# A hybrid decoder layer: rope in two halves, the sums of w_out moved behind the attention, casts and squares placed apart

## The chip, the cores and the metric

The kernel runs on one core of a Trainium2 chip. The metric is device time in microseconds (us), the median of three runs; lower is better. One more execution was taken by the hardware profiler, and all views quoted here are of that one. Its engines are PE (TensorE: matrix products), DVE (VectorE), ACT (ScalarE), POOL (GpSimd) and SP (SyncE, which here only issues transfers); 16 DMA engines move data.

## The reference, cut to what matters

One decoder layer on x of 512 tokens by 1024 channels, in float32. Two branches run on the same normed input and are merged by gates.

```python
h    = rms_norm(x, norm_g)
proj = h @ w_in            # q | f | i | z_a | c_q | c_kv | k_rope | z_b | gate logits (2 x 1024)
y_a  = hgrn2_branch(hq, hf, hi, hz, ...)       # 8 heads of 128, chunkwise gated recurrence
y_b  = mla_branch(cq, ckv, kr, mz, ...)        # 8 heads of 128 + 64 rope, causal attention
gates  = sigmoid(glog + b_gate)                # two gates per channel
merged = gates[0] * (y_a @ w_proj_a) + gates[1] * (y_b @ w_proj_b)
out    = rms_norm(x + merged @ w_out, final_norm_g)
```

Rope turns the 64 rope channels of each query head: `[x1*cos - x2*sin, x2*cos + x1*sin]`, so the two 32-channel halves have to be exchanged.

## The kernel before, in words

**Precision.** Every float32 operand of a product is split in two float32r parts, hi and lo, and a product is made of three matmuls, hi*hi, hi*lo and lo*hi (`mm3`, lines 88 to 93). `load_w` (lines 99 to 120) brings 0.5 MB of a weight into a buffer `w_raw` by SP (line 112), ACT casts it to `w_hi` (line 118) and DVE subtracts to get `w_lo` (line 119). There are three buffers of `w_raw` and four each of `w_hi` and `w_lo`. `split` (lines 160 and 161) does the same for an operand made on the chip.

**Stages.** (1) Norm, transposes into hT, the low-rank projections cT. (2) HGRN2 in four pairs of heads (`hg_pair`): forget, value or gate, query products, then states, scores, outputs. (3) Attention, head by head (lines 904 to 934): `mla_scores`, `mla_gate`, `mla_nope` for the next head, `mla_transpose`, `mla_out`; every second head `mla_rope` for the next two. (4) Two gate products, (5) the product with `w_proj_a`, each by Strassen's scheme with seven half-size products (`strassen`, lines 871 to 895), (6) the plain product with `w_proj_b`, (7) the Strassen-like product with `w_out`, the residual and the final norm.

**Sums of weight blocks.** Strassen needs four sums of 512x512 blocks for each of the four matrices (`gate_w[0]`, `gate_w[1]`, `pa_w`, `out_w`; class `BlockSums`, lines 736 to 763). They are made in DRAM by the DMA engines alone: `start` queues eight copies of 0.5 MB from the weight to a DRAM tile (`g_t`, `pa_t`, `out_t`); `load_w` issues one of the queued copies on SP behind each weight load (lines 113 to 115, 747). `add` then issues accumulating transfers of 0.5 MB on POOL (line 754), two for each of the four sums: n = 0 and 2 add a block of the weight, n = 1 and 3 add an earlier sum. `out_t` of n = 1 therefore waits for n = 0, and n = 3 for n = 1.

**What sets the order.** Within an engine a scheduler orders the instructions by its own model of time, unless a stretch is in `manual_schedule`, which keeps the order of the code for the engines named. The list `adds` (lines 796 and 797) is popped by `step()`, 11 times in HGRN2 and once for each of heads 1 to 6 of the attention; all four matrices are started before HGRN2 (line 805). In `strassen` the work on the coming operands (`between`: `a_parts` and others) is put in with `issue_after(last_lo)` (line 877), so on DVE it stands behind the last `w_lo` of the weight just loaded.

**Rope.** `mla_rope(pair)` (lines 622 to 642) makes the product for two heads, copies it to `qr` (ACT, line 626), sends four transfers of 64 KB from ACT's queue to exchange the quarters (`qs`, line 628), multiplies and adds on POOL (lines 629 to 631), sends two transfers of 128 KB (line 635) and casts into `qp` and `qh` (lines 637 to 641). For pair 0 it is called in `first_scores` (line 815), behind the states of the last pair of HGRN2, and for pairs 1 to 3 behind the scores of heads 1, 3 and 5 (lines 908 to 910).

**End.** `squares_of` (line 1069) takes its scratch `sq` from the three `w_raw` buffers.

Of the kernel before, what the change touches and what calls it, by code (L numbers as in the profile page):

```python
# [9 lines left out]
F32 = mybir.dt.float32  # L10
# [8 lines left out]
P = 128  # L19
# [4 lines left out]
H = 8  # L24
# [10 lines left out]
WCH = 1024  # L35
# [3 lines left out]
def hybrid_layer(ctx: ExitStack, tc: tile.TileContext, a):  # L39
    nc = tc.nc  # L40
# [4 lines left out]
    wraw = ctx.enter_context(tc.tile_pool(name="wraw", bufs=3))  # L45
# [14 lines left out]
    def z_tile():  # L60
        return zpool.tile([P, S], F32, tag="z", name="z")
# [31 lines left out]
        nc.tensor.matmul(ps, ll[lsl], rh[rsl], start=False, stop=stop)  # L93

    last_dma = [None]
    last_lo = [None]
    queued = []

    def load_w(*pieces, to=None):

        raw = wraw.tile([P, WCH], F32, tag="raw", name="w_raw")
        hi, lo = to or [pool.tile([P, WCH], F32R, tag=tag, name=f"w_{tag}")[:] for pool, tag in ((whi, "hi"), (wlo, "lo"))]
        views, o = [], 0
        for src in pieces:
            n = int(np.prod(src.shape[1:]))
            if len(src.shape) == 4:
                _, k, h, c = src.shape
                dst = raw[:, o : o + n].rearrange("p (k h c) -> p k h c", k=k, h=h)
                for i in range(k):
                    nc.sync.dma_start(dst[:, i], src[:, i])  # L110
            else:
                last_dma[0] = nc.sync.dma_start(raw[:, o : o + n].rearrange("p (k c) -> p k c", k=src.shape[1]), src)
                if queued:
                    with tc.issue_after(last_dma[0].ins):
                        queued.pop(0)()
            views.append([t[:, o : o + n].rearrange("p (k c) -> p k c", k=src.shape[1]) for t in (hi, lo)])
            o += n
        nc.scalar.copy(hi[:, :o], raw[:, :o])  # L118
        last_lo[0] = nc.vector.tensor_tensor(lo[:, :o], raw[:, :o], hi[:, :o].bitcast(F32), op=ALU.subtract)  # L119
        return views[0] if len(views) == 1 else views  # L120

# [159 lines left out]
    with tc.manual_schedule(engines={mybir.EngineType.PE, mybir.EngineType.Activation, mybir.EngineType.DVE}):  # L281
# [17 lines left out]
        sq, rs = st.tile([P, D], F32, "sq", bufs=2), rss[0]  # L299
# [316 lines left out]
    def low(w, k0, nk):  # L616
        ps = mm_tile()
        for k in range(nk):
            mm3(ps[:], w, cT, (slice(None), k), (slice(None), k0 + k), k == 0, k == nk - 1)
        return ps  # L620

    def mla_rope(pair):

        ps = low(load_w(w_uq[:, :, 2 * pair : 2 * pair + 2, 128:192]), 0, 3)
        qr, qs = ma_pool.tile([P, S], F32, "qr"), ma_pool.tile([P, S], F32, "qs")
        nc.scalar.copy(qr[:], ps[:])
        for b in range(4):
            nc.scalar.dma_start(qs[32 * b : 32 * b + 32, :], qr[32 * (b ^ 1) : 32 * (b ^ 1) + 32, :])
        nc.gpsimd.tensor_tensor(qr[:], qr[:], qtab[:, 0], op=ALU.mult)
        nc.gpsimd.tensor_tensor(qs[:], qs[:], qtab[:, 1], op=ALU.mult)  # L630
        nc.gpsimd.tensor_tensor(qr[:], qr[:], qs[:], op=ALU.add)

        qx = ma_pool.tile([P, S], F32, "qs")
        for i in range(2):
            nc.scalar.dma_start(qx[64 * i : 64 * i + 64, :], qr[64 - 64 * i : 128 - 64 * i, :])
        qp, qh = [ma_pool.tile([P, S], F32R, f"qp{i}") for i in range(2)], ma_pool.tile([P, S], F32R, "qh")
        nc.scalar.copy(qh[:], qx[:])
        for i in range(2):
            own, other = slice(64 * i, 64 * i + 64), slice(64 - 64 * i, 128 - 64 * i)
            nc.scalar.copy(qp[i][own], qr[own])  # L640
            nc.vector.tensor_tensor(qp[i][other], qx[other], qh[other].bitcast(F32), op=ALU.subtract)
        return qp
# [86 lines left out]
    def minus(out, x, y):  # L729
        nc.vector.tensor_tensor(out, x, y, op=ALU.subtract)  # L730
# [34 lines left out]
    gate_w = [BlockSums(f"g{b}", w_in[:, COL_G + b * D : COL_G + b * D + D]) for b in range(2)]  # L765
    pa_w = BlockSums("pa", a["w_proj_a"][0])
    out_w = BlockSums("out", a["w_out"][0])
    h_dram = [[dram.tile([P, 4, 256], F32, name=f"h{n}{i}") for i in range(2)] for n in range(1, 5)]

    def early_sums(q):  # L770
# [9 lines left out]
        def keep(n, tag, src):  # L780
# [12 lines left out]
        minus_minus(e12, e12, e22)  # L793
        keep(4, "qn", e12)

    adds = [(gate_w[0], 0), (gate_w[0], 2), (gate_w[0], 1), (gate_w[1], 0), (gate_w[0], 3), (gate_w[1], 2), (gate_w[1], 1),
            (pa_w, 0), (gate_w[1], 3), (pa_w, 2), (pa_w, 1), (out_w, 0), (pa_w, 3), (out_w, 2), (out_w, 1), None, (out_w, 3)]

    def step():
        if adds and last_pool[0]:  # L800
            x = adds.pop(0)
            if x:
                x[0].add(x[1])

    for w in (*gate_w, pa_w, out_w):
        w.start()

    for pair in range(H // 2 - 1):
# [3 lines left out]
    early = []  # L812

    def first_scores():
        early.append(mla_rope(0))
        early.append(mla_nope(0, ma_pool))

    def last_outputs(scores, outs, gated):
# [5 lines left out]
            gated(on)  # L824
        return z

    z = hg_pair(H // 2 - 1, first_scores, last_outputs)
    hw.close()

# [41 lines left out]
    def strassen(w, ops, out, pool, first=None, between={}):  # L871

        y11, y12, y22, s1, s2, s3, s4 = ops

        def run(n):
            if n in between:
                with tc.issue_after(last_lo[0].ins):
                    between[n]()

        if first is None:  # L880
            u = ch_product(w.block(0, 0), y11, copied("c11", 1.0, pool))
            run(1)
            ch_product(w.block(1, 0), y12, closed("c11", 0, 0, 1.0, out), tile=mm_tile)
            run(2)
        else:
            u = first
        r = ch_product(w.sum(1), s1, copied("c22", -1.0, pool))
        run(3)
        ch_product(w.sum(2), s2, copied("c12", -1.0, pool), u)
        run(4)  # L890
        ch_product(w.block(1, 1), s4, closed("c12", 4, 0, -1.0, out), r)
        run(5)
        ch_product(w.sum(3), s3, closed("c22", 4, 1, -1.0, out), u)
        run(6)
        ch_product(w.sum(4), y22, lambda b, ps: out(2 * b, 1, two(ps)), u)
# [6 lines left out]
    qp, nope, pn = early  # L902
    late = None
    for h in range(H):
        pools = (ma_pool, mw)
        if h:
            pn = mla_scores(h, pools[h % 2], *nope, qp, h + 1 == H)
        if h + 1 < H:
            if h % 2:
                qp = mla_rope((h + 1) // 2)  # L910
        if h:
            z = mla_gate(h)
        if h:
            if h + 1 < H:
                nope = mla_nope(h + 1, pools[(h + 1) % 2])
            mla_out(*late)
            if h % 4 == 0:
                v = mla_values(h)
        hook = lambda: mla_transpose(pn)
        if h + 1 == H:  # L920
            with tc.manual_schedule(engines={mybir.EngineType.PE}):
                pts, later = [], []
                w11, w21 = gate_w[0].block(0, 0), gate_w[0].block(1, 0)
                u = ch_product(w11, h11, copied("c11", 1.0))
                ch_product(w21, h12, lambda b, ps: later.append((b, ps)), tile=mm_tile, hook=lambda: pts.extend(hook()))
                mla_out(h, pts, v, z)
        elif h:
            late = (h, hook(), v, z)
            step()
        else:  # L930
            with tc.manual_schedule(engines={mybir.EngineType.PE}):
                nope = mla_nope(1, pools[1])
                v = mla_values(0)
                late = (0, hook(), v, z)
# [25 lines left out]
        closed("c11", 0, 0, 1.0, gate_out(0, lambda j: ma[:, j]))(b, ps)  # L960
    h_ops = (h11, h12, h22, s1, s2, s3, s4)
    y11, y12, y21, y22 = blocks(ya)
    with tc.manual_schedule(engines={mybir.EngineType.PE}):
        strassen(gate_w[0], h_ops, gate_out(0, lambda j: ma[:, j]), gp, first=u,
                 between={3: lambda: a_parts(y11, q1), 4: lambda: a_parts(y12, q2), 5: lambda: a_parts(y22, q3),
                          6: lambda: [minus(y22[:, q], y22[:, q], y21[:, q]) for q in kh]})
    g1 = {j: z_tile()[:] for j in (0, 1, 4)}
    for n, j in enumerate((2, 3, 5, 6, 7)):
        g1[j] = g_rows[:, n]
# [51 lines left out]

    sp = Pool("sums", "left")
    s1, s2 = [[sp.tile([P, 4, 256], F32R, f"s{n}{i}") for i in range(2)] for n in (1, 2)]
    fg = [z_tile() for _ in range(2)]
    with tc.issue_after(xr_in.ins):
        for n in range(2):
# [41 lines left out]

    def squares_of(t, i, o, n):

        sq = wraw.tile([P, WCH], F32, tag="raw", name="sq")
        nc.scalar.activation(sq[:, :n], xr[t][:, o : o + n], AF.Square, scale=D ** -0.5, accum_out=ssum[:, t, i : i + 1])  # L1072
        if t > 1:
            nc.vector.tensor_tensor(rgs[t - 2][:, o : o + n], xr[t][:, o : o + n], fg[o // 512][:, o % 512 : o % 512 + n],
                                    op=ALU.mult)
# [119 lines left out]
```

## Time and profile before

| | us |
|---|---|
| three runs: median (lowest to highest) | 627.75 (627.64 to 627.92) |
| the profiled execution, its own time | 626.55 |
| its span, first to last instruction | 624.8 |
| PE busy in the span | 603.7 |
| DVE / ACT / POOL busy | 431.9 / 284.6 / 147.7 |
| granted PE clock, mean | 0.996 of full speed |

The span is what the views divide up; 1.75 us of the profiled execution's time lie around it. The profile's page has the busy time of each engine, the span in 40 slices with a digit for tenths, the DMA queues (q1 is SP's, q10 ACT's, q0 POOL's), and groups of instructions. "Share of 16 engines" is the time that a queue's packets took, as a share of what 16 DMA engines have. A view of waits names who waited for whom, with total, number and longest; the view of DMA can be asked for a window. In a row of the timeline the brackets hold the idle time of the engine before the instruction and what ended it. L844 is the matmul of the Strassen products, L91 to L93 are the three of `mm3`.

### The profile page before, as it was taken

What the parts mean: (1) busy time and instruction counts of PE and PEld (TensorE: products, weight loads), DVE (VectorE), ACT (ScalarE), POOL (GpSimd) and SP (SyncE); (2) the same over time, 40 slices, a digit from 0 to 9 for tenths busy, and PEclk for the clock granted to TensorE, in tenths of its full rate; (3) what the DMA queues carried; (4) which work ended last, traced back from release to release, by engine and by line L of the source; (5) the groups of instructions that cost most, each with busy time, mean ns of one, the idle gap of its engine ahead of it and who ended that gap; (6) DMA issues with size and microseconds to landing.
All of it is one profiled execution on the core that took longest, in us unless ns stands there. A gap on an engine that the chain in (4) does not pass through costs nothing.

```text
span 624.8 us, 9801 instructions
## 1 busy us (share of the span) xinstructions
PE 603.7 (97%) x3688; PEld 526.9 (84%) x3688; DVE 431.9 (69%) x679; ACT 284.6 (46%) x531; POOL 147.7 (24%) x245
## 2 busy tenths in 40 slices
PE   8999999999999999979998999898999999999994
PEld 5998888888888888867887888798999999888883
DVE  7727989498864459838665766655766687657886
ACT  5645244323233232346555454437677844333352
POOL 3106322444341153351525213320000000000012
PEclk9999999999999999999999999999999999999998
DMA  7449479988979944937575662584656555685043
GB/s 250 166 140 335 152 244 367 277 207 183 285 128 342 220 62 116 195 98 151 96 150 121 125 161 84 135 311 162 205 170 198 194 165 183 203 302 169 1 134 135
DMA packets 74799, 114.37 MB, mean 183 GB/s; under 512 B 7512, under 2 KB 41726, under 8 KB 74752
## 3 DMA queue, kind: packets, MB, share of 16 engines
q1 hardware_dynamic: 65100, 89.69, 44.3%
q0 software_dynamic: 7952, 21.50, 19.2%
q10 hardware_dynamic: 1700, 2.56, 1.4%
q8 instruction: 29, 0.48, 0.3%
q14 instruction: 18, 0.15, 0.1%
HBM read 105.34 MB, written 39.85 MB: 232 GB/s over the span
## 4 chain that ended last, share of the span: by engine, by line
PE 78%; DVE 8%; DMA 4%; ACT 4%; issue 3%; POOL 2%; ACTq 0%; POOLq 0%; SPq 0%; DVEq 0%
PE mm_ps L91 16%; PE mm_ps L92 16%; PE mm_ps L93 16%; PE ax_ps L844 16%; PE mm_ps L844 3%; DMA qs<-qr 2%; DVE w_lo L119 2%; PE mm_ps L271 1%; PE ax_ps L687 1%; PE ax_ps L711 1%; DMA w_raw<-w_uq 1%; DVE ya L1067 1%; PE ax_ps L541 1%; PE ax_ps L91 1%; PE ax_ps L93 1%
## 5 line engine op out<-in xcount | busy, mean ns | idle before, releaser
L119 DVE TENSOR_TENSOR w_lo<-w_raw,w_hi 128x1024 fp32r<-128x1024 f32 (+3 forms) x116 | 137.1, 1194 | 91.2 <-ACT w_hi L118 85.4
L118 ACT CAST w_hi<-w_raw 128x1024 fp32r<-128x1024 f32 (+3 forms) x116 | 114.9, 1004 | 141.5 <-PE mm_ps L92 60.8
L91 PE MATMUL mm_ps<-hT,w_hi 128*128 128x512 f32 x320 | 126.0, 395 | 0.4 <-DVE qn L161 0.4
L92 PE MATMUL mm_ps<-hT,w_hi 128*128 128x512 f32 x320 | 125.1, 391 | 0.0
L93 PE MATMUL mm_ps<-hT,w_lo 128*128 128x512 f32 x320 | 124.7, 392 | 0.0
L91 PEld LDWEIGHTS mm_ps<-hT,w_hi 128*128 128x128 f32 x320 | 60.2, 188 | 12.5 <-DVE qn L161 0.6
L93 PEld LDWEIGHTS mm_ps<-hT,w_lo 128*128 128x128 f32 x320 | 60.1, 188 | 12.4
L92 PEld LDWEIGHTS mm_ps<-hT,w_hi 128*128 128x128 f32 x320 | 60.1, 188 | 11.8
L844 PE MATMUL ax_ps<-s,w_hi 128*128 128x256 f32 x384 | 54.2, 283 | 2.1 <-ACT w_hi L118 2.1
L844 PEld LDWEIGHTS ax_ps<-s,w_hi 128*128 128x128 f32 x384 | 49.6, 192 | 2.5 <-ACT w_hi L118 2.5
L1085 POOL TENSOR_SCALAR ssum<-ssum 128x1 f32<-128x1 f32 x3 | 0.9, 316 | 185.8 <-ACT sq L1072 185.8
L93 PE MATMUL mm_ps<-w_hi,hT 128*128 128x512 f32 (+1 forms) x96 | 36.6, 383 | 0.0
L92 PE MATMUL mm_ps<-w_lo,hT 128*128 128x512 f32 (+1 forms) x96 | 36.5, 382 | 0.0
L91 PE MATMUL mm_ps<-w_hi,hT 128*128 128x512 f32 (+1 forms) x96 | 36.4, 386 | 0.0
L844 PE MATMUL ax_ps<-s,w_lo 128*128 128x256 f32 x192 | 31.3, 284 | 0.2 <-DVE w_lo L119 0.2
L695 POOL TENSOR_SCALAR p<-p,sm 128x128 f32<-128x128 f32 (+3 forms) x28 | 16.8, 604 | 61.5 <-DVE sm L692 51.6
L693 ACT ACTIVATE p<-ax_ps,sm 128x128 f32<-128x128 f32 (+3 forms) x32 | 16.9, 529 | 27.7 <-DVE sm L692 26.3
L844 PEld LDWEIGHTS ax_ps<-s,w_lo 128*128 128x128 f32 x192 | 26.6, 192 | 0.4 <-DVE w_lo L119 0.4
L460 DVE RECIPROCAL tf<-pr 128x512 f32<-128x512 f32 x8 | 26.8, 3348 | 0.1
L91 PE MATMUL mm_ps<-cT,w_hi 128*128 128x512 f32 x52 | 20.7, 398 | 0.0
L93 PEld LDWEIGHTS mm_ps<-w_hi,hT 128*128 128x128 f32 x96 | 18.0, 188 | 3.0
L91 PEld LDWEIGHTS mm_ps<-w_hi,hT 128*128 128x128 f32 x96 | 18.0, 188 | 3.0
(296 smaller groups left out, 1205.5 us busy)
## 6 DMA issues: line engine op xcount, KB each, us to landing
w_raw<-w_in SPq DMA_DIRECT2D x54, 512.0 KB, 6.9
g_t<-w_in SPq DMA_DIRECT2D x16, 512.0 KB, 8.9
w_raw<-g_t SPq DMA_DIRECT2D x16, 512.0 KB, 4.2
g_t<-w_in POOLq DMA_DIRECT2D x8, 512.0 KB, 11.3
pa_t<-w_proj_a SPq DMA_DIRECT2D x8, 512.0 KB, 12.2
g_t<-g_t POOLq DMA_DIRECT2D x8, 512.0 KB, 8.3
out_t<-w_out SPq DMA_DIRECT2D x8, 512.0 KB, 8.9
s<-h POOLq DMA_DIRECT2D x8, 512.0 KB, 7.5
```

Of the source, the lines that this page charges most:

```text
L91: nc.tensor.matmul(ps, lh[lsl], rh[rsl], start=start, stop=False)
L92: nc.tensor.matmul(ps, lh[lsl], rl[rsl], start=False, stop=False)
L93: nc.tensor.matmul(ps, ll[lsl], rh[rsl], start=False, stop=stop)
L118: nc.scalar.copy(hi[:, :o], raw[:, :o])
L119: last_lo[0] = nc.vector.tensor_tensor(lo[:, :o], raw[:, :o], hi[:, :o].bitcast(F32), op=ALU.subtract)
L271: nc.tensor.matmul(ps, hT[l][:, 4 * kh + k, t * P : t * P + P], c_hl[kh][r][:, k * 256 : k * 256 + 256], start=kh == 0 and kind == 0 and k ...
L460: nc.vector.reciprocal(rp[:], pr[:])
L541: nc.tensor.matmul(ops[:, sl], asb[:, sl], v_sb[i][:, (h % 4) * P : (h % 4) * P + P], start=True, stop=i == 0)
L687: nc.tensor.matmul(sps[:, :n], qh[:, bl], kpe[x][:, :n], start=False, stop=x == 1)
L693: nc.scalar.activation(p[:, :n], sps[:, :n], AF.Exp, scale=SCALE, bias=sm[:, 1:2], accum_out=sm[:, 2:3])
L695: scaled_p = (nc.vector if final else nc.gpsimd).tensor_scalar(p[:, :n], p[:, :n], sm[:, 3:4], 0.5, op0=ALU.mult, op1=ALU.mult)
L844: nc.tensor.matmul(ps[:, o], w[k // 2][i][:, k % 2, cols], ap[j][:, k], start=not banks and c == 0 and n == 0, stop=n == 11, skip_group_ch ...
```

## The change

It has four parts.

1. `mla_rope` becomes `mla_turn(pair)` (product, copy, exchange, POOL's arithmetic, second transfers) and `mla_rope(qr, qx)` (the casts). The turn for pair 0 is issued ahead of the last pair of HGRN2; for pairs 1 to 3 ahead of the scores of heads 1, 3 and 5, and the casts behind those scores.
2. `out_w` is started only before the first gate product, so its eight copies follow the first eight weight loads of that stage, and its adds are issued behind the code of that product. `adds` is left with the eight of the gates in another order, the adds of `pa_w` are made at heads 2 (n = 0 and 2), 4 (n = 1) and 6 (n = 3).
3. The work in `between` is held behind the last cast to `w_hi` on ACT as well.
4. `sq` gets a tile of its own.

```diff
-        nc.scalar.copy(hi[:, :o], raw[:, :o])
+        last_hi[0] = nc.scalar.copy(hi[:, :o], raw[:, :o])
...
-    def mla_rope(pair):
+    def mla_turn(pair):
 
         ps = low(load_w(w_uq[:, :, 2 * pair : 2 * pair + 2, 128:192]), 0, 3)
...
         for i in range(2):
             nc.scalar.dma_start(qx[64 * i : 64 * i + 64, :], qr[64 - 64 * i : 128 - 64 * i, :])
+        return qr, qx
+
+    def mla_rope(qr, qx):
+
...
-    adds = [(gate_w[0], 0), (gate_w[0], 2), (gate_w[0], 1), (gate_w[1], 0), (gate_w[0], 3), (gate_w[1], 2), (gate_w[1], 1),
-            (pa_w, 0), (gate_w[1], 3), (pa_w, 2), (pa_w, 1), (out_w, 0), (pa_w, 3), (out_w, 2), (out_w, 1), None, (out_w, 3)]
+    adds = [(gate_w[0], 0), (gate_w[0], 2), (gate_w[1], 0), (gate_w[0], 1), (gate_w[1], 2), (gate_w[0], 3), (gate_w[1], 1),
+            None, (gate_w[1], 3)]
...
-    for w in (*gate_w, pa_w, out_w):
+    for w in (*gate_w, pa_w):
         w.start()
...
-        early.append(mla_rope(0))
+        early.append(mla_rope(*turned_q))
...
+    turned_q = mla_turn(0)
     z = hg_pair(H // 2 - 1, first_scores, last_outputs)
...
-                with tc.issue_after(last_lo[0].ins):
+                with tc.issue_after(last_lo[0].ins), tc.issue_after(last_hi[0].ins):
...
+        if h % 2 and h + 1 < H:
+            turned_q = mla_turn((h + 1) // 2)
         if h:
             pn = mla_scores(h, pools[h % 2], *nope, qp, h + 1 == H)
-        if h + 1 < H:
-            if h % 2:
-                qp = mla_rope((h + 1) // 2)
+        if h % 2 and h + 1 < H:
+            qp = mla_rope(*turned_q)
...
-            step()
+            if h % 2 == 0:
+                pa_w.add(*{2: (0, 2), 4: (1,), 6: (3,)}[h])
...
+    out_w.start()
     with tc.manual_schedule(engines={mybir.EngineType.PE}):
         strassen(gate_w[0], h_ops, gate_out(0, lambda j: ma[:, j]), gp, first=u,
...
+    out_w.add(0, 2)
+    out_w.add(1)
+    out_w.add(3)
...
+    sq = sp.tile([P, 512], F32, "sq")
...
-        sq = wraw.tile([P, WCH], F32, tag="raw", name="sq")
```

How this moves instructions, at three places. A number behind a tile's name tells buffers apart: `g_t_647` and `g_t_648` are the first and second sum of the first gate's weight, `out_t_659` to `out_t_662` the four of `w_out`, `h_663` and on the stored sums of the activations. Lines are those of each kernel's own file; L751 and L758 of the changed kernel are L747 and L754 of before, L950 is L943.

SP's queue where the first gate product begins, in the kernel before: the last load of the attention, the four loads of the two plain blocks, then the sums.

```order
L112 DMA w_raw<-w_in 128x8x128
L112 DMA w_raw<-w_in 128x2x512 x4
L112 DMA w_raw<-g_t_647 128x1024 x2
L112 DMA w_raw<-g_t_648 128x1024 x2
L112 DMA w_raw<-w_in 128x2x512 x2
L112 DMA w_raw<-g_t_649 128x1024 x2
```

The same place in the changed kernel.

```order
L112 DMA w_raw<-w_in 128x8x128
L112 DMA w_raw<-w_in 128x2x512 x4
L112 DMA w_raw<-g_t_647 128x1024
L751 DMA out_t_659<-w_out 128x2x512
L112 DMA w_raw<-g_t_647 128x1024
L751 DMA out_t_659<-w_out 128x2x512
L112 DMA w_raw<-g_t_648 128x1024
L751 DMA out_t_660<-w_out 128x2x512
L112 DMA w_raw<-g_t_648 128x1024
```

A copy of 0.5 MB now stands behind each of eight weight loads in a row; it goes on so up to the second load of `g_t_649`.

POOL's queue from the last probabilities of the attention to the end, before:

```order
L695 TENSOR_SCALAR p_3946<-p_3946,sm 128x512
L754 DMA out_t_662<-out_t_660 128x1024 x2
L943 DMA s_4339<-h_663 128x1024
L943 DMA s_4340<-h_664 128x1024
...
L943 DMA s_4344<-h_668 128x1024
L1085 TENSOR_SCALAR ssum<-ssum 128x1 x2
```

and in the changed kernel:

```order
L699 TENSOR_SCALAR p_3930<-p_3930,sm 128x512
L758 DMA pa_t_658<-pa_t_656 128x1024 x2
L950 DMA s_4323<-h_663 128x1024
...
L950 DMA s_4328<-h_668 128x1024
L758 DMA out_t_659<-w_out 128x2x512 x2
L758 DMA out_t_660<-out_t_659 128x1024 x2
L758 DMA out_t_661<-w_out 128x2x512 x2
L758 DMA out_t_662<-out_t_660 128x1024 x2
L1096 TENSOR_SCALAR ssum<-ssum 128x1 x2
```

All eight adds of `w_out` now stand behind the loads of the activations' sums, one after the other, with nothing of POOL behind them until the final norm.

ACT's queue where rope of pair 0 stands, in the last pair of HGRN2, before (`osq` are the squares of the recurrence's outputs, `kt` is of its states):

```order
L626 COPY qr<-mm_ps 128x512
L628 DMA qs<-qr 32x512 x3
L499 COPY kt<-ax_ps 128x384
L628 DMA qs<-qr 32x512
...
L635 DMA qs<-qr 64x512 x2
L640 CAST qp_2574<-qr 64x512
L640 CAST qp_2575<-qr 64x512
L118 CAST w_hi<-w_raw 128x1024
L637 CAST qh<-qs 128x512
L547 ACTIVATE osq,ss<-ax_ps 128x128 x8
```

In the changed kernel it stands ahead of the squares of the pair before, which start at 221.16 us of the profiled span, where the L626 of the rows above starts at 254.48 us (`tf` belongs to the forget gates of the last pair):

```order
L626 COPY qr<-mm_ps 128x512
L628 DMA qs<-qr 32x512 x4
L547 ACTIVATE osq,ss<-ax_ps 128x128 x8
L118 CAST w_hi<-w_raw 128x1024
L635 DMA qs<-qr 64x512 x2
L454 ACTIVATE tf<-mm_ps 128x512
L644 CAST qp_2562<-qr 64x512
L644 CAST qp_2563<-qr 64x512
L118 CAST w_hi<-w_raw 128x1024
L641 CAST qh<-qs 128x512
```

The squares of the last pair no longer stand behind the transfers and casts of rope.

More of the change, by code (lines that the diff above doesn't have):

```diff
@@ L95, in hybrid_layer @@
     last_dma = [None]
-    last_lo = [None]
+    last_hi, last_lo = [None], [None]
     queued = []
```

## The prediction

> **What bounds the kernel now.** I read the page first: busy time by engine, then the slices.
>
> ```profile
> PE 603.7 (97%) x3688; PEld 526.9 (84%) x3688; DVE 431.9 (69%) x679; ACT 284.6 (46%) x531; POOL 147.7 (24%) x245
> ...
> PE   8999999999999999979998999898999999999994
> ...
> DMA  7449479988979944937575662584656555685043
> ```
>
> PE has work in 97% of the span, and only the slices around 265, 335, 405, 425 and the end fall below 9. So whatever moves on other engines counts only where PE waits. The view of PE's waits lists them; the columns are line of PE, what released it, total us, number, longest.
>
> ```profile
> PE ax_ps L687 <- DVE qp L641: 2.5, 1, 2.5
> PE ax_ps L844 <- ACT w_hi L118: 2.1, 2, 1.6
> PE ax_ps L91 <- DVE pt L161: 1.6, 1, 1.6
> PE ax_ps L711 <- POOL p L695: 1.4, 1, 1.4
> ...
> PE mm_ps L91 <- DVE z L563: 1.1, 1, 1.1
> PE ax_ps L1033 <- DVE ya L1067: 0.8, 1, 0.8
> ...
> PE ax_ps L91 <- DVE k L549: 0.7, 1, 0.7
> ...
> PE ax_ps L844 <- DVE w_lo L119: 0.2, 1, 0.2
> ```
>
> These rows, 10.4 us together, are about all that removing waits can bring; the tail behind the last matmul is not touched. Each part of the change aims at one of them. What a part can cost is a new wait where PE has none today: the Strassen stages.
>
> **Rope of pair 0.** The chain of waits between 258 and 278 us (start, us, what):
>
> ```profile
> 258.28 8.68 DMA qs<-qr
> 267.12 1.26 POOL qr L629
> ...
> 274.43 0.61 ACT qh L637
> 275.05 0.27 ACT osq L547 x2
> ...
> 277.37 1.04 POOL ss L166
> ```
>
> The exchange of quarters takes 8.68 us, POOL's arithmetic follows, then ACT's casts, and only behind them on ACT the squares `osq`, which the last pair's outputs need. So three of PE's waits hang on this one transfer: 2.5 for `qp`, 0.7 for `k` (L549, released by the squares) and 1.1 for `z`. In the changed kernel the turn and its casts are over a whole pair earlier. All three go: 2.5 + 0.7 + 1.1 = -4.3 us. Its nine matmuls, six transfers and three POOL operations now lie in slices where PE shows 9 and the add of `pa_w` that was there is gone; ACT's second transfers wait for POOL with the tanh of the forget gates behind them, which PE's full queue hides. I take 0 for that; without the cover it would be the three operations' 3 x 1.3 = 4 us.
>
> **Rope of pair 1 and the adds at head 2.** POOL's timeline there:
>
> ```profile
> 320.16 1.68 POOL L754 DMA_DIRECT2D pa_t<-pa_t  x2
> ...
> 332.34 1.29 POOL L629 TENSOR_TENSOR qr<-qr,qtab 128x512 f32<-128x512 f32 x1 [2.70 <-DMA qs<-qr]
> ...
> 337.52 1.25 POOL L695 TENSOR_SCALAR p<-p,sm 128x384 f32<-128x384 f32 x2
> ```
>
> Two adds are issued at 320.2, rope's exchange comes behind them, POOL stands until 332.3, and probabilities queued behind rope on POOL are late: PE's 1.4 us at L711. The change puts four adds there in place of two, so the exchange has adds beside it for longer. Between -1.4 (the earlier product helps) and +4.5 (it waits about as much longer as half of another pair): I take +1.
>
> **The copies and adds of `w_out`.** Until now they ran beside HGRN2 and the attention. Taking them away there brings 0, as PE shows no wait there that they cause but those above. They come to the first gate product, whose need the view of DMA for 440 to 480 us shows (packets, MB, share of 16 engines):
>
> ```profile
> DMA packets 2803, 7.45 MB, mean 186 GB/s; under 512 B 224, under 2 KB 224, under 8 KB 2799
> ...
> q1 hardware_dynamic: 2799, 7.40, 58.7%
> ...
> w_raw<-g_t SPq DMA_DIRECT2D x8, 512.0 KB, 3.8
> ```
>
> 7.40 MB are 14.1 loads of 0.524 MB in 40 us: one in 2.83 us, with a landing time of 3.8 us, and 41% of the DMA engines left over. What an add costs stands in the same view for 145 to 169 us, where four adds (q0) met SP's queue (q1):
>
> ```profile
> q0 software_dynamic: 832, 2.10, 54.2%
> q1 hardware_dynamic: 2545, 3.79, 48.7%
> ...
> w_raw<-w_in SPq DMA_DIRECT2D x4, 512.0 KB, 13.4
> ```
>
> The engines are full (103%). Four adds took 0.542 x 24 = 13.0 us of them, 3.25 each; SP's 3.79 MB are 7.2 transfers in 11.7 us, 1.62 each; and a weight load landed after 13.4 us. In HGRN2 PE bears that: there it is four loads in 24 us, one in 6, not one in 2.83. New work in the gate stage: eight adds, 8 x 3.25 = 26.0, and six copies (the first two go out before the adds can start), 6 x 1.62 = 9.7; 35.7 us in all. In a stretch of L us the leftover 41% takes in 0.41 L. Nothing holds the adds back but their own copies and sums; at the pace of the rows above four take 24 us, so L = 48, and short are 35.7 - 0.41 x 48 = 16 us.
>
> How much of that the loads' lead covers, from ACT's and DVE's timelines and the chain:
>
> ```profile
> 453.03 2.00 ACT L118 CAST w_hi<-w_raw 128x1024 fp32r<-128x1024 f32 x2 [1.36 <-issue]
> ...
> 458.74 2.00 ACT L118 CAST w_hi<-w_raw 128x1024 fp32r<-128x1024 f32 x2 [1.50 <-PE ax_ps L844]
> ```
> ```profile
> 454.11 2.36 DVE L119 TENSOR_TENSOR w_lo<-w_raw,w_hi 128x1024 fp32r<-128x1024 f32 x2 [2.00 <-ACT w_hi L118]
> ```
> ```profile
> 459.42 5.76 PE mm_ps L844 x48
> ```
>
> The weights of the product that starts at 459.42 are ready at 456.5: 3 us of lead. The next cast is released by PE, not by its load, so the data lay ready; I allow 1.5 us more, 4.5 in all. PE then loses 16 - 4.5 = 11.5 us. The 2.3 us that PE waits here already (L844 for `w_hi` and `w_lo`) lie in the same stretch and are not paid twice: +9 us. Bounds: if the adds took only what the loads leave, -2.3; if they take as many bytes as SP's queue, an add and a transfer take 4.87 us, L is 39, short are 19.7, and it is +12.9.
>
> The Trainium skill (DMA: Bandwidth & Descriptors, "Queues, rings and completion order") says that each engine serves the queue rows in turn, one packet from each; by that rule the adds get as many turns as SP's queue, and the sum takes the upper bound, +12.9. The row has 2545 packets of SP's beside 832 of POOL's, so here the turns were not one to one over the stretch as a whole, and I keep 9.
>
> **Casts held on ACT.** ACT's timeline where PE waits for `w_hi`:
>
> ```profile
> 424.49 3.21 ACT L160 CAST q<-ya 128x512 fp32r<-128x512 f32 x6
> ...
> 428.09 1.98 ACT L118 CAST w_hi<-w_raw 128x1024 fp32r<-128x1024 f32 x2
> ```
>
> Six operand casts stand before two weight casts that PE needs. The new order would take out up to the 2.3 us; the operands themselves are wanted only in the product with `w_proj_a`, so their delay costs 0. But with loads late it is the load that PE waits for, so in my sum this brings nothing of its own.
>
> **Squares.** SP's queue waits for `sq` here:
>
> ```profile
> SPq L112 <- ACT sq L1072: 1.2, 2, 1.0
> ```
>
> The last weights come up to 1.2 us earlier, but PE's 0.8 us there is for DVE's L1067, not for a weight. Between 0 and -0.8; I take 0.
>
> **Sum.** -4.3 + 1 + 9 = +5.7 us on the profiled execution's 626.55. The median of the runs is 627.75, 1.2 above it; I add the difference to the median: 633.5 us. With the gate stage between +7 and +12 and rope of pair 1 between -1.4 and +4, this case spans 629 to 639.
>
> **Rivals.** (1) *The gate stage takes it in.* The adds yield, the copies fit between loads, and the held casts bring their 2.3: 627.75 - 4.3 - 2.3, with 1.4 more at best from pair 1 and the squares: about 620.5. For it: the 41% left over, and nobody needs the sums before the product with `w_out` 100 us later. Against it: the adds would have to stretch over (35.7 - 4.5) / 0.41 = 76 us, 19 for each pair, where the rows show 12. (2) *Half of the shortage*: adds are held up by late copies, L is about 62, short are 10, less lead and old wait +3.5; with -4.3 and +1, 628. (3) *Worse*: one turn each (+12.9), and four adds in front of pair 1's exchange (+4.5): 627.75 - 4.3 + 17.4, about 641. (4) *Rope's early half hides nothing*, because ACT or POOL makes the early place pay the same 4.3: 638.
>
> **Chances.** Likeliest case 0.40, (1) 0.30, (2) 0.12, (3) 0.13, (4) 0.05. The likeliest case alone is 629 to 639. The range reaches into (1) and (3): 620 to 641, which leaves out the better part of (1) and of (3), less than 2 in 10. A measurement of this kernel can tell about 0.2%, 1.3 us, from no change. Faster by more: (1) and a quarter of (2), 0.33; within: 0.05; slower by more: 0.62.
>
> **What would show it.** Right: no wait of PE for `qp` (L687), `k` or `z` near 275 us; in the first gate product waits of PE at L844 for `w_hi` and `w_lo` of over 8 us together, released by loads that land after 8 us or more instead of 3.8; DMA digits of 9 from about 400 to 460 us; the later stages as dense as now, only shifted. Wrong: `w_raw<-g_t` still landing near 4 us while adds run, and PE's slices at 9 there; then it is rival (1) and the time is near 620.

## The result, and the profile after

| | before | changed | 
|---|---|---|
| median of the runs, us (lowest to highest) | 627.69 (626.68 to 627.92) | 642.23 (641.72 to 647.03) |
| the profiled execution / its span, us | 626.55 / 624.8 | 642.71 / 640.8 |

The changed kernel takes 1.025 of the time of before (95% interval 1.020 to 1.030): 14.5 us slower, where 5.7 were forecast, and 1.2 us above the range. The page of the changed kernel, busy time and slices (L849 here is L844 of before, L715 is L711, L1045 is L1033):

```profile
PE 609.8 (95%) x3688; PEld 533.7 (83%) x3688; DVE 433.1 (68%) x679; ACT 285.6 (45%) x531; POOL 147.0 (23%) x245
...
PE   8999999999999999999989999947799999999994
...
PEclk9999999999999999999999999987899999999999
DMA  7549399969695523504393825999976555685123
```

The slice at 265 us is full now. The hole is at 417 to 465 us, the first gate product, where the DMA engines show four nines in a row and the granted clock falls. PE's waits say for what:

```profile
PE ax_ps L849 <- ACT w_hi L118: 16.0, 4, 7.4
PE ax_ps L715 <- POOL p L699: 2.4, 2, 1.6
...
PE ax_ps L1045 <- DVE ya L1079: 0.9, 1, 0.9
PE ax_ps L849 <- DVE part L872: 0.8, 1, 0.8
```

The waits for `qp`, `k` and `z` are gone, and 2.1 us for `w_hi` have become 16.0. The view of DMA for 415 to 460 us shows weight loads that land after 14 us, where those of the kernel before take 4.4 (408 to 449 us):

```profile
q1 hardware_dynamic: 3209, 7.66, 53.5%
q0 software_dynamic: 1604, 3.95, 50.1%
...
w_raw<-g_t SPq DMA_DIRECT2D x5, 512.0 KB, 14.2
out_t<-w_out SPq DMA_DIRECT2D x5, 512.0 KB, 18.0
```

SP's queue, which has loads and copies, and POOL's, which has the adds, each hold half of engines that are full.

**Where the time went.** PE runs the same 3688 matmuls in these kernels, near the marks used here in the same order, so their start times can be set against each other, counted from the last one. The 1380th from the end lies in the first of the seven half-size products of the first gate product, the 1080th in the last of them; worked out from the matmul starts of the two traces:

```
                       before   changed   difference so far
1380th from the end    409.77    403.99   -5.8
1080th                 449.18    465.10   +15.9
last                   616.89    632.93   +16.0
```

Up to the gates the changed kernel is 5.8 us ahead; between the two marks it loses 21.7 us (61.1 us in place of 39.4); from there to the end the gap doesn't change. The same stretch in the view by windows (its columns: window, length, busy us of PE, PEld, DVE, ACT and POOL with counts, then granted clock, DMA share, GB/s), first of the kernel before, then of the changed one:

```profile
409.77:449.18 39.41, 37.11 (x302) 36.36 (x301) 23.61 (x29) 23.68 (x38) 1.15 (x3) 1.00 0.70 236
```
```profile
403.99:465.10 61.11, 44.32 (x303) 43.01 (x301) 23.57 (x30) 22.38 (x36) 9.02 (x10) 0.83 1.03 275
```

Share times length is engine time: 0.70 x 39.41 = 27.6 us before, 1.03 x 61.11 = 62.9 us now. The new work is therefore 35.3 us; 35.7 were forecast. (Some 1.6 of the 35.3 are loads of the activations' sums, 4.19 MB behind the mark now and 3.60 before.) So the work was priced right in total, and what it costs PE was not. A share counts the time that packets took, their waiting included; whether the engines or the memory behind them are the limit, no run here separates. The clock is a second suspect: PE's busy time in the stretch is 7.2 us longer at a clock of 0.83.

### The profile page after: what moved, and what is told of

Its sections match the earlier page's. It is cut to its first block, busy times and chain, and to the rows that moved or that the text cites. A ratio compares the mean times of both kernels' runs of the same rounds, so it can differ in the third digit from the quotient of the medians.

```text
span 640.8 us, 9797 instructions
## 1 busy us (share of the span) xinstructions
PE 609.8 (95%) x3688; PEld 533.7 (83%) x3688; DVE 433.1 (68%) x679; ACT 285.6 (45%) x531; POOL 147.0 (23%) x245
## 4 chain that ended last, share of the span: by engine, by line
PE 80%; DMA 7%; DVE 5%; ACT 3%; issue 2%; POOL 2%; ACTq 1%; POOLq 0%; DVEq 0%
PE mm_ps L91 17%; PE mm_ps L92 17%; PE mm_ps L93 17%; PE ax_ps L849 14%; DMA w_raw<-w_in 3%; PE mm_ps L849 3%; DMA w_raw<-g_t 2%; DMA qs<-qr 2%; PE mm_ps L271 1%; PE ax_ps L691 1%; DVE w_lo L119 1%; PE ax_ps L541 1%; PE ax_ps L715 1%; PE ax_ps L236 1%; PE ax_ps L503 1%
## 5 line engine op out<-in xcount | busy, mean ns | idle before, releaser
L849 PE MATMUL ax_ps<-s,w_hi 128*128 128x256 f32 x384 | 59.8, 301 | 16.0 <-ACT w_hi L118 16.0
L91 PEld LDWEIGHTS mm_ps<-hT,w_hi 128*128 128x128 f32 x320 | 60.1, 188 | 12.3 <-DVE qn L161 0.6
L93 PEld LDWEIGHTS mm_ps<-hT,w_lo 128*128 128x128 f32 x320 | 60.1, 188 | 12.3
L92 PEld LDWEIGHTS mm_ps<-hT,w_hi 128*128 128x128 f32 x320 | 60.1, 188 | 11.8
L849 PEld LDWEIGHTS ax_ps<-s,w_hi 128*128 128x128 f32 x384 | 54.6, 209 | 16.8 <-ACT w_hi L118 16.8
L849 PE MATMUL ax_ps<-s,w_lo 128*128 128x256 f32 x192 | 33.2, 297 | 0.0
L699 POOL TENSOR_SCALAR p<-p,sm 128x128 f32<-128x128 f32 (+3 forms) x28 | 15.2, 545 | 65.5 <-DVE sm L696 33.2
L849 PEld LDWEIGHTS ax_ps<-s,w_lo 128*128 128x128 f32 x192 | 28.6, 206 | 0.2 <-DVE w_lo L119 0.2
L91 PE MATMUL mm_ps<-cT,w_hi 128*128 128x512 f32 x52 | 20.7, 398 | 0.0
## 6 DMA issues: line engine op xcount, KB each, us to landing
pa_t<-w_proj_a SPq DMA_DIRECT2D x8, 512.0 KB, 12.9
```

The source lines that it names most:

```text
L91: nc.tensor.matmul(ps, lh[lsl], rh[rsl], start=start, stop=False)
L92: nc.tensor.matmul(ps, lh[lsl], rl[rsl], start=False, stop=False)
L699: scaled_p = (nc.vector if final else nc.gpsimd).tensor_scalar(p[:, :n], p[:, :n], sm[:, 3:4], 0.5, op0=ALU.mult, op1=ALU.mult)
L849: nc.tensor.matmul(ps[:, o], w[k // 2][i][:, k % 2, cols], ap[j][:, k], start=not banks and c == 0 and n == 0, stop=n == 11, skip_group_ch ...
```

## The experiments

Theory at the start: the engine time in that stretch is the whole cause (A). Rivals: the order on SP's queue, each load behind a copy (Q); the clock, halved after PE's waits (C); a cost hidden in the other parts. All kernels are edits of the changed one unless another is named. For each the stretch between the same two marks is given, worked out from matmul starts as above:

```
                                      1380th   1080th   stretch
before                                409.77   449.18   39.4
changed                               403.99   465.10   61.1
part 2 undone                         408.06   445.40   37.3
no adds of w_out                      404.08   445.41   41.3
copies early, adds behind the sums    406.10   455.44   49.3
rope halves alone                     410.03   450.49   40.5
part 2 undone, casts not held         407.98   447.39   39.4
adds of the attention regrouped       409.56   446.89   37.3
```

**Part 2 undone.**

```diff
-    for w in (*gate_w, pa_w):
+    for w in (*gate_w, pa_w, out_w):
...
-            if h % 2 == 0:
-                pa_w.add(*{2: (0, 2), 4: (1,), 6: (3,)}[h])
+            step()
...
-    out_w.start()
...
-    out_w.add(0, 2)
-    out_w.add(1)
-    out_w.add(3)
```

with the list `adds` of before.

> The changed kernel with part 2 undone (w_out started before HGRN2, and the list of adds as before); the rope halves, the held casts and the tile of sq stay. Theory (the loss lies in the gate stage alone, and comes from the transfers of w_out): the gate stage's idle time (16.75 us) and PE's slower matmuls there (6.1 us more busy time) go, and 627.7 - 4.3 (rope) - 2.3 (old waits of the gate stage) give about 621, 619.5 to 623. Rival (the other parts have a cost of their own that the trace puts down to the gate stage, the held casts above all): 627 or more, with waits for w_hi at the gate stage still there.

Measured 623.48 us (622.73 to 626.83), 0.994 of before (0.992 to 0.997), half a us above the theory's range: the loss is part 2's, and this kernel beats both. It takes 37.3 us for the stretch, 2.1 less than before. But it is only 1.7 us ahead at the 1380th matmul, not 5.8; its waits have a new row:

```profile
PE mm_ps L91 <- DVE z L563: 1.8, 1, 1.8
PE ax_ps L91 <- DVE pt L161: 1.6, 1, 1.6
```

The first lies at 242 us, at the place that rope of pair 0 has moved to; the second was in the kernel before at 401.8 us. Neither is in the changed kernel. So ahead of the gates part 2 is worth 408.06 - 403.99 = 4.1 us. That is not the transfers of `w_out` alone, none of whose adds runs in HGRN2: part 2 also moves the adds of `w_proj_a` out of HGRN2, two of which are issued at 231.2 and 232.0 us here and land by 243.5, just where `z` is late. The two runs with early copies (below) have the copies of `w_out` in HGRN2 but not these adds, and no wait for `z`. The wait for `pt` goes with the order of PE's matmuls in the last head: the kernel before, this one and the others with that wait have one order there, the changed kernel and all runs without the wait another.

**No adds.** The three lines `out_w.add(...)` removed; the sums of `w_out` are left as plain blocks.

> The changed kernel without the eight adds of w_out (its sums are left as plain blocks; the eight copies between the weight loads stay). Theory A (the time of the DMA engines decides: eight adds at 3.25 us are some 26 of about 30 us that the stretch has too much): what is left, six to eight copies of 1.6 us, fits into what the loads leave, loads land after 4 to 7 us, and the time is 621 to 626. Rival Q (the order on SP's queue decides: each of eight weight loads stands behind a copy of 0.5 MB): more than half of the loss stays, 632 or more, with loads landing after 8 us or more.

Measured 622.59 us (622.19 to 623.65). The stretch, beside PE's waits in it:

```profile
404.08:445.41 41.33, 38.96 (x302) 37.91 (x301) 24.08 (x31) 22.91 (x37) 1.03 (x2) 0.96 0.91 311
```
```profile
PE ax_ps L849 <- ACT w_hi L118: 2.3, 3, 1.6
```

Eight copies stand between the loads as they did, and cost 41.3 - 37.3 = 4 us of the 61.1 - 37.3 = 23.8 that copies and adds cost together. Q falls. The copies are 0.91 x 41.33 - 0.76 x 37.34 = 9.2 us of engine time (0.76 is the share in the stretch of the kernel without part 2). The forecast has 9.7 for six of them; that its total came out is luck in this part:

```profile
408.06:445.40 37.34, 36.86 (x303) 36.31 (x301) 23.87 (x31) 23.56 (x38) 1.20 (x3) 1.00 0.76 249
```

**Filled waits.** Extra matmuls where PE waits for the second half of a weight:

```diff
+                    if n_fill and (b, c, n) == (0, 0, 2):
+                        for _ in range(n_fill):
+                            nc.tensor.matmul(idle_ps[:, o], hT[0][:, 0, 0:128], hT[0][:, 0, 0:256], start=True, stop=True)
...
+    FILL = (56, 48, 36)
```

> The changed kernel with 56, 48 and 36 extra matmuls of 128x256 (about 0.116 us each, on data that lie ready, into a bank that nobody reads) on PE in the second, third and fourth half-size product of the first gate product, where PE waits for the second half of the weight: 6.5, 5.6 and 4.2 us of work in place of idle time, so that PE is never idle for long and the granted clock should stay at 1.0. Theory A (loads set the pace there): the time stays at 641 to 644; the waits that are left and the fillers together grow as the matmuls get faster. Rival C (the halved clock costs its 6.1 us of slower matmuls on its own): 635 to 638.

Measured 645.19 us (642.16 to 648.25), far from C's 635 to 638 and 1.2 us above A's range. The changed kernel by windows of 5 us, then this one:

```profile
425.00:430.00 5.00, 0.00 (x0) 0.00 (x0) 0.00 (x0) 0.00 (x0) 0.86 (x1) 0.64 1.02 263
430.00:435.00 5.00, 3.68 (x17) 3.69 (x18) 2.43 (x3) 2.09 (x3) 0.81 (x1) 0.50 1.05 295
...
445.00:450.00 5.00, 5.00 (x25) 5.00 (x25) 2.31 (x5) 1.70 (x4) 1.13 (x1) 0.50 1.06 265
```
```profile
425.00:430.00 5.00, 5.00 (x44) 5.00 (x43) 0.49 (x1) 1.57 (x3) 0.86 (x1) 1.00 1.05 333
430.00:435.00 5.00, 5.00 (x44) 5.00 (x43) 1.94 (x3) 0.52 (x1) 0.81 (x1) 1.00 1.06 307
...
460.00:465.00 5.00, 0.72 (x3) 0.75 (x4) 3.65 (x4) 3.10 (x7) 0.00 (x0) 0.76 0.82 192
```
```profile
PE ax_ps L856 <- DVE part L880: 4.9, 1, 4.9
```

At the halved clock 25 matmuls take the 5 us that 44 take at full clock. With the fillers the clock holds at 1.00 to 460 us, and PE is done earlier only to wait longer, 4.9 us on one wait at the end of the stretch. No time is won, so C falls: while loads are late here, slow matmuls fill time that PE would stand. The 642.2 of the changed kernel lie at the lower end of this run's spread, so the fillers themselves may have cost up to 3 us.

**One product later.** `out_w.start()` and the three adds moved to the second gate product, where the loads leave more of the engines free.

> The changed kernel with the start of w_out and its adds one product later: the eight copies follow the first eight loads of the second gate product, the adds stand behind that product's code. There the kernel before keeps the DMA engines busy for 0.58 of the time (446 to 486 us), beside the first gate product for 0.71 (408 to 446 us). Theory A (what counts is the engine time that is left over, with some 30 us of new work over 55 us): PE gets (55 - 30) / 0.58 = 43 us of work done in those 55, loses about 12, less 4.5 of lead, so about 7.5 to 12 above the kernel without part 2 (about 621): 628 to 633. Rival (the adds slow a weight load by the same factor wherever they meet one): 640 or more, as now.

Measured 641.57 us (639.4 to 643.49), the rival's number: theory A in this form falls. The stretch between the marks and the next 420 matmuls (the second gate product and the first part of the product with `w_proj_a`) of this kernel, and below them the latter of the kernel without part 2:

```profile
403.98:441.39 37.41, 36.94 (x303) 36.40 (x302) 23.96 (x31) 22.81 (x37) 2.34 (x4) 1.00 0.81 270
441.39:515.19 73.80, 59.49 (x422) 58.43 (x421) 34.63 (x40) 35.80 (x57) 6.76 (x7) 0.86 0.89 233
```
```profile
445.40:495.80 50.40, 50.40 (x423) 50.40 (x421) 33.99 (x40) 34.77 (x57) 0.00 (x0) 1.00 0.59 187
```

New work: 0.89 x 73.80 - 0.59 x 50.40 = 36 us. The leftover there is 0.41 x 50.4 = 20.7, so 15 us should be lost; lost are 73.8 - 50.4 = 23.4. The engines were not full over the 73.8 us, but they were while the adds ran, from 440 to 493 us:

```profile
q1 hardware_dynamic: 3811, 8.82, 52.1%
q0 software_dynamic: 1664, 4.19, 47.0%
```

The adds took about half of the engines although the loads needed them, and were done in 53 us. What the loads leave free after that is of no use. So theory A became P: the cost is settled in the time in which the adds run; of that stretch L the loads get what copies and adds (W) leave, and at a demand d PE gets (L - W) / d of its work done. Here (53 - 36) / 0.59 = 29 us of work in 53, a loss of 24. P is made from this run; the next ones test it.

**Copies early.** `w_out` started before HGRN2, the adds left where they are.

> The changed kernel with w_out started before HGRN2 as in the kernel before, so that its eight copies run beside HGRN2 and the attention; only the eight adds stay in the gate stage. Theory P (while the adds run one behind the other, they and the loads fill the DMA engines, and engine time that the loads lack is paid by PE at the rate at which PE uses loads): copies and adds together cost PE 23.8 us against the kernel without part 2, at 0.92 x 37.4 = 34.5 us of new engine time; without the copies (9.2 us) 25.3 us are left, some 10 to 14 us of loss, so 632 to 636. Rival E (the adds alone make the loads late, and the copies cost nothing beside them): 640 or more. Rival Q (a load is late because a copy goes ahead of it on SP's queue): 627 or less.

Measured 637.37 us (637.16 to 638.97), above P's range, and the run tells nothing for P: with the copies done, the adds went to POOL's queue ahead of the loads of the activations' sums, and PE waited 11.1 us for `s`. The same with the adds held behind those loads (`last_pool[0] = nc.gpsimd.dma_start(s[i][:], ...)`):

> The run with early copies again, with the eight adds of w_out held on POOL behind the loads of the activations' sums, where the changed kernel has them (in the run before they stood ahead of those loads, and PE waited 10.4 us for s). Theory P as before: 25.3 us of engine time for the adds and 28.4 for the stage's own transfers, beside 37.4 us of PE's work; if the adds take 48 to 57 us, the loads get what is left of that stretch, (48 - 25.3) to (57 - 25.3) us, worth 30 to 42 us of PE's time at 0.76, so PE loses 15 to 18 us, less up to 4 of lead, against the kernel without part 2: 632 to 637, with waits for w_hi at L849 alone. Rival E (the copies cost nothing beside the adds): 640 or more. Rival Q (a load is late because a copy goes ahead of it on SP's queue): 627 or less.

Measured 633.29 us (632.35 to 634.29), in P's range, partly by luck: the range was worked out for adds that take 48 to 57 us, and they took 45 (408.9 to 453.9). For 45 the formula gives a loss of 45 - (45 - 25.3) / 0.76 = 19 us, less up to 4 of lead, where the stretch shows 12; for the changed kernel (57 us, 34.5 of new work) it gives 27, where 23.8 were lost. So P overshoots. Nor is half a fixed share: from 418 to 454 us POOL's queue has 60.1% of the engines here and SP's 38.7%. Stretch and waits:

```profile
406.10:455.44 49.34, 40.33 (x303) 39.20 (x301) 23.47 (x30) 22.88 (x37) 8.95 (x10) 0.93 1.02 269
```
```profile
PE ax_ps L849 <- ACT w_hi L118: 7.2, 3, 4.0
...
PE ax_ps L849 <- DVE part L872: 1.7, 1, 1.7
```

The adds alone cost 49.3 - 37.3 = 12 us, the copies alone 4, both 23.8: more than the sum, as work does that shares engines which one of the two already fills.

**Spread adds.** The eight adds go out one by one, each behind a small POOL copy that waits for the `w_lo` of a weight load: at every fourth load from the ninth on; then at every third from the eighteenth on, with a copy of `w_out` behind every second load only.

```diff
+        if loads[0] is not None:
+            loads[0] += 1
+            if paced and loads[0] >= every[2] and (loads[0] - every[2]) % every[1] == 0:
+                turn = nc.gpsimd.tensor_copy(pace, lo[:, 0:1].bitcast(F32))
+                with tc.issue_after(turn.ins):
+                    paced.pop(0)()
```

> The changed kernel with the same eight copies and eight adds of w_out, but each add is held on POOL behind a copy of one column out of the w_lo of every fourth weight load, from the ninth load of the first gate product on, so that they spread over both gate products and the product with w_proj_a (some 80 us instead of 57). Theory P (the loss is that of a stretch in which work comes faster than the engines have time left over): an add of 3.25 us every 11 us needs 0.29 of the engines where the loads leave 0.41, so what is left is the cost of the copies; 621 to 625. Rival E (each of the eight adds makes the loads beside it late, at 2.5 us of PE each, wherever it stands): 638 or more.

> The same with the copies spread too: one copy behind every second weight load, adds from the eighteenth load on at every third. Theory P: the copies no longer meet the loads of the activations' sums at the head of the first gate product all at once, their 2.3 us of waits there and 1.7 us of slower matmuls shrink, and the time is 618 to 622, below the kernel before and the kernel without part 2 (623.5). Rival (the cost of the copies is a fixed one for each load that has one ahead): 622.5 or more; adds that end too late for the product with w_out would show as waits at its loads, 630 or more.

Measured 631.61 us (628.34 to 636.74) and 626.39 us (622.93 to 630.99). Spreading brings back 10.6 and 15.8 us, so no add has a fixed price of 2.5 us of PE, and E falls. But both miss P's ranges; the second time is one that its rival (a fixed cost for each load with a copy ahead, 622.5 or more) allows. DMA of the first of the two, from 444.9 to 532.5 us:

```profile
w_raw<-g_t SPq DMA_DIRECT2D x8, 512.0 KB, 6.3
...
w_raw<-w_proj_a SPq DMA_DIRECT2D x6, 512.0 KB, 6.2
out_t<-out_t POOLq DMA_DIRECT2D x4, 512.0 KB, 8.8
```

Its engines are busy for 0.77 of that window, and still each add, which lands after about 9 us, makes the loads beside it land after 6 instead of the 4 of the kernel without part 2. Counted from the kernel without part 2, PE is 4.0 us ahead at the 1380th matmul and 8.0 us behind at the last, so 12 are lost: 4 if the copies cost what they did without adds, and then some 1.0 for each add. An average over the stretch doesn't see that; P is a rule for adds in a row, and the price of a single add is left open.

**Rope halves alone**, on the kernel before, all else as there.

> The kernel before with the rope in two halves alone (part 1; all transfers of w_out and their places as before, no held casts, sq as before). Theory of the forecast: PE's waits for qp, k and z near 275 us go, 4.3 us, and with the earlier product for pair 1 up to 1.4 more: 622 to 623.5. Rival (with the adds of w_out still issued in HGRN2 the exchange at its new place waits for them, and the z wait at 242 us of the kernel without part 2 takes its place): about 1.7 us gain, 625 to 626.

Measured 627.32 us, 1.000 of before (0.998 to 1.003), above the theory's range and the rival's. No gain: the three waits at 275 us went, and these came (0.4 of the wait for `qn` was there before):

```profile
PE mm_ps L91 <- DVE z L563: 1.8, 1, 1.8
...
PE mm_ps L91 <- DVE qn L161: 0.8, 1, 0.8
PE ax_ps L503 <- ACT kt L499: 0.6, 1, 0.6
```

By waits the early half still gains about 1 us; the profiled execution lost that to the clock, which was at 0.50 from 338.6 us on for 3.4 us, and the runs show no gain. The text of the rival has the adds of `w_out` beside the exchange; in the trace of this place they are those of `w_proj_a`, as for the kernel without part 2. Part 2 takes them away, and with them the wait for `z`; between 200 and 250 us the DMA engines are busy for 0.70 here, and 0.41 in the changed kernel. Which of the transfers that are gone matters most was not tried one by one.

**Casts not held**, on the kernel without part 2: `with tc.issue_after(last_lo[0].ins):` as before.

> The kernel without part 2 (rope halves, tile of sq, adds as before), and without part 3: the work on the operands is held behind the last w_lo on DVE alone, as before. Theory (the held casts bring the 2.1 us of PE's waits for w_hi and w_lo at the first gate product, where the loads are in time): 625 to 626.5, with waits of 1.6 and 0.4 us at L849. Rival (the waits go for another reason, the earlier casts change nothing): 623.5, as with the held casts.

Measured 626.92 us (625.1 to 630.95) beside 623.48 with the casts held. Its profiled span is 623.3 beside 621.3, and the stretch 39.4 us beside 37.3; the old wait is back:

```profile
PE ax_ps L849 <- ACT w_hi L118: 2.1, 2, 1.6
```

So the held casts are worth 2 us where the loads are in time: with them and no transfer of `w_out` beside it the stretch takes 37.3 us (also with the adds regrouped, below), without them 39.4 to 40.5. The medians differ by 3.4 us, within the spread of both.

**Adds of the attention regrouped**, an attempt at a better version.

```diff
-            if h % 2 == 0:
-                pa_w.add(*{2: (0, 2), 4: (1,), 6: (3,)}[h])
+            for w, n in {1: ((pa_w, 0), (pa_w, 2)), 3: ((pa_w, 1), (out_w, 0)), 4: ((out_w, 2),),
+                         5: ((pa_w, 3), (out_w, 1)), 6: ((out_w, 3),)}.get(h, ()):
+                w.add(n)
```

> The changed kernel with w_out started before HGRN2 again and all adds of w_proj_a and w_out made during the attention, none in HGRN2's last pair: w_proj_a n = 0 and 2 at head 1, n = 1 and w_out n = 0 at head 3, w_out n = 2 at head 4, w_proj_a n = 3 and w_out n = 1 at head 5, w_out n = 3 at head 6, each held on POOL behind the rope of the pair before as well, so that no exchange is issued behind two pairs of adds. Theory (the 4.1 us by which the changed kernel is ahead of the kernel without part 2 at the first gate product come from adds that no longer meet the exchanges of rope; the gate stage itself needs none of them): 618.5 to 621.5, below the kernel before and the kernel without part 2. Rival (the adds cost PE their 4 us wherever they run beside the attention): 623 to 625.

Measured 625.16 us (621.41 to 627.98), 0.996 of before (0.994 to 0.999): the theory missed, and the time is just above the rival's 623 to 625. The gate stage is as good as without part 2 (37.3), but rope of pair 3, with four adds issued beside it at 375 to 377 us, is late in turn:

```profile
PE ax_ps L691 <- DVE qp L645: 2.6, 1, 2.6
PE ax_ps L91 <- DVE pt L161: 1.6, 1, 1.6
```

The best version here is the kernel without part 2.

## Why the prediction came out as it did

**Right.** The direction; that the place is the first gate product with waits at L849 for `w_hi` of over 8 us (16.8 with `part`), loads that land after 14 us, DMA digits of 9 from 400 to 464 us, and later stages that are only shifted. Rope of pair 0: the three waits of 4.3 us are gone, and one of 0.6 (`kt`) has come. The waits for `p` and `qn` are 2.4 + 0.3 now, 1.4 + 0.4 before, so +0.9 where +1 was forecast; that is luck as to the place, as pair 1 pays 1.6 for 1.4 and a new wait of 0.7 lies at pair 2 (373 us). (POOL did not stand from 320 to 332.3 us, as the prediction reads the row: it worked at 329.3 and waited 2.7 us for the exchange.) The new DMA work: 35.3 us measured, 35.7 forecast, right in total. Casts: nothing here, as the late loads come first, and 2 us where they don't. Squares: nothing, PE's last wait is for DVE's L1079 as it was.

**Wrong: "in a stretch of L us the leftover 41% takes in 0.41 L".** That step gave 0.41 x 48 = 19.7 us for free. Three things are wrong with it. The 41% were read at 440 to 480 us; the adds start at 408, where the eight loads of the activations' sums come too and the stretch before has 30% left. The 48 us are a time with PE's waits in it; leftover exists only for the 39.4 us of the kernel's own pace: 0.30 x 39.4 = 11.8 us. And the second gate product, with its 41%, did no better: the adds don't take what is left, they take about half or more, and the row quoted for 145 to 169 us in the prediction says so (q0 54.2%, q1 48.7%).

**Wrong: 4.5 us of lead.** The engines were full from the first mark to the second, so the stretch lasts as long as the work moved in it: with the forecast's own 35.7 us, (27.6 + 35.7) / 1.03 = 61.5 us, 22.1 more than 39.4, and 21.7 were measured. No 4.5 us come off. All the lead that the traces show is what was put off behind the second mark: in the next 50.4 us the engines are busy for 0.63 now and 0.58 before, 2.5 us of work that cost PE nothing; the 35.3 are already net of it. Put right in these two terms, the forecast's +9 becomes 9 + (19.7 - 11.8) + 4.5 = 21.4. The 2.3 us taken off for the old waits were in order: against the kernel without part 2, which has 0.4 us of such waits, the stretch is 23.8 us longer, against before 21.7.

**Mis-sized: "taking them away there brings 0".** Part 2 brought 4.1 us ahead of the gates (part 2 undone). With the copies of `w_out` put back alone some 1.5 to 2.1 of them are lost again (the 1380th matmul starts at 405.44 and 406.10 in the two runs with early copies, one trace each): that much the term is off. The rest goes with the adds of `w_proj_a` and with the order of PE's matmuls, and the shares are not separated further. PE's waits of before were put down to rope's exchange alone; with the adds of `w_proj_a` left in place the exchange pays 1.8 us for `z` at its new place, and rope alone gains nothing. So the early half's -4.3 belongs to parts 1 and 2 together.

**The sum by the measured terms.** -5.8 up to the gates (forecast -3.3) and +21.7 in them (forecast +9) make +15.9; the spans differ by 16.0. Of the -5.8, 4.3 and 1.6 (`pt`) went, 0.9 and 0.6 came; the last 1.4 are not followed. Rival (3) came nearest, with 641, but by luck: pair 1 paid hardly anything extra instead of 4.5, and the gates 21.7 instead of 12.9. Its one turn each is not what the rows show, with 3209 packets of SP's queue to 1604 of POOL's, though their shares of the engines are nearly equal. Rival (1), that the gate stage takes the work in, needed adds over 76 us; they took 57, from 408.5 to 465.7 us. Rival (4) comes near for the rope halves alone, where 3.4 us of waits came for the 4.3 that went, and is wrong beside part 2.

## What to carry to other kernels

A transfer that "has time" took half of the engines at once here: before work is moved under a stage, compute the stage by engine time (share x length of the same work, before), and allow the leftover only for the time in which the moved transfers run and PE works. Lead of prefetched loads did not shorten a stretch in which the engines were full throughout. And a wait put down to one transfer may belong to the traffic around it: the edit that thins the traffic and the edit that moves the transfer have to be tried apart.

## What the runs showed of the hardware

The granted clock fell to half behind quite short waits, and not always. The kernel with the rope halves alone and the one without held casts have the same two waits at the first gate product, 2.1 us together (the row shown above stands in both), within 2.6 us by the matmul starts. The windows just behind them, first of the rope halves, then of the other:

```profile
430.00:434.00 4.00, 3.62 (x18) 3.62 (x19) 4.00 (x5) 1.76 (x3) 0.00 (x0) 0.60 0.54 161
```
```profile
428.00:432.00 4.00, 3.44 (x26) 3.24 (x27) 4.00 (x5) 1.70 (x3) 0.00 (x0) 1.00 0.57 165
```

The first is at 0.60 of the clock and gets 18 matmuls done, the second at 1.00 and 26; the stretch is 40.5 us in the one and 39.4 in the other. The Trainium skill (TensorE: Matmul & The Clock Gate, "What's actually happening") has the clock fall to half after an idle window of about 3.4 us. The changed kernel agrees in two of its three falls (waits of 7.4 and 4.5 us; the third, at 457 us, follows one of 2.4), but here 2.1 us of waiting were enough once and not the other time. It shows in the spread of one kernel's runs too: the 23 runs of the kernel before beside the last three experiments go from 625.0 us at a mean clock of 0.997 to 629.4 at 0.988. Where loads paced PE, keeping the clock up won nothing (the filled waits); where they don't, each short wait has this risk on top.
